# Rotary products on VectorE, early weight columns, and three smaller moves in a two-layer hybrid decoder trunk

## The chip, the core and the metric

The kernel runs on one core of a Trainium2 chip. The metric is the device time of one execution in microseconds. TensorE (PE) multiplies, VectorE (DVE), ScalarE (ACT) and GpSimd (POOL) work on tiles in SBUF, and the first two also on the accumulators in PSUM. SyncE (SP) issues most of the DMAs. An engine takes its instructions in order, and semaphores order the engines among one another.

## The reference

Two layers (DEPTH 2) on 1024 tokens of width 1024, all in float32:

```
h = RMSNorm(x); p = h @ W_in                       # columns for all branches
branch A: u * (tril(W_s) LayerNorm(v) + b) per 128-token chunk, 4 groups
branch B: window-128 attention, 8 query / 2 key heads of 64, rotary q and k, sinks
branch C: stick-breaking attention, 4 heads of 128, strictly causal
each branch * SiLU(its gate) @ its W_branch; merged with sigmoid gates from h
x <- x + RMSNorm(merged @ W_out)
```

The rotary of a head is `x1*cos - x2*sin, x2*cos + x1*sin` on its two halves.

## The kernel before

**Products.** Every operand of a large product is held as two tiles, a high part `hi` rounded to a shorter format and the rest `lo`, and `mm3` (L128 to L130) makes one product of three matmuls: hi hi, hi lo, lo hi. `split` (L111, L112) makes the pair: ScalarE casts the high part, VectorE subtracts it from the raw value. Both layers run the same program.

**Order.** The order on PE is the order of the program text, written by hand; on the other engines a scheduler orders the instructions by readiness and priority, and what stands under `tc.high_priority()` goes first. The projection of h is a stream of jobs (`proj_t` for 128 columns, 16 steps of cost 0.64, and `proj_n` for 256 columns, 64 steps of 0.32). `fill(us)` runs steps of that stream until their costs reach the sum given, `need(label)` runs it until a job is done, so that attention products and projection products alternate on PE. The jobs follow one another: branch C's columns, k and v of branch B (`kb`, `vb`), its four query pairs (`qb` 0 to 3), the gates `gb` 0 to 3, then the value columns of branch A (`va`). A job's accumulator is one of two PSUM tiles `pj`, emptied by its `evac`, which also starts what follows (`after_q`, `rope`).

**Memory.** Most of SBUF is 27 slots of 128 x 1024 words, handed out by `new()` from the head of a queue and put back at its tail by `done()`. Whoever gets a slot waits until its last user is through. Weight columns come through two buffers `wr` and six operand buffers `w` (whi, wlo, wop).

**Start.** `first_h` norms the eight token blocks of x; `norm_b` transposes a block on PE into a PSUM tile (pz), ScalarE copies it to `raw` (L238), and `split` makes both parts of h from PSUM (L239).

**Branch B.** `rope` copies the tile t with swapped halves into sw by four DMAs (L292), multiplies sw by sin and t by cos on POOL (L293, L294) and adds on VectorE (L295); then `after_q` makes hi and lo (L346, L347) and frees t. `scores` makes 4 x 256 score columns in each of two PSUM tiles (L486), from which ScalarE copies the own block (L492, L493, L498) and VectorE the previous one under a mask (L496, L499); then softmax on VectorE and ScalarE (L503 to L511, exponentials L507). `transp` transposes the weights, `attend` multiplies them with v (L543) and adds two halves (L553, L554) through a temporary slot. Scores run two blocks ahead; the numbers FB are the fills between the pieces.

**Dense part.** After branch B, `dense` computes 17 pairs of 128-column groups by a scheme of seven products for eight. `prep(p)` makes a pair's seven weight operands (wop) from the raw columns, four combinations by POOL (L748 to L758), up to six operands ahead of the products; `begin(p)` loads the raw columns as two halves, each 512 KB. VectorE adds the products (L818). Ahead of the loop stand the sums of h that the scheme needs (`Combine`) and, among its first pairs, branch A's normalisation (L615 to L621).

**End.** `project_out` multiplies by W_out in two column halves; the second pass norms each block of 128 tokens, adds x and stores it.

Of the kernel before, what the change touches and what calls it, by code (L numbers as in the profile page):

```python
# [15 lines left out]
F32 = mybir.dt.float32  # L16
# [3 lines left out]
ALU = mybir.AluOpType  # L20
AX = mybir.AxisListType

P = 128
# [10 lines left out]
O_M = 4864  # L34
NSLOT = 27
FC = (0.6, 0.6, 1.2, 0.6)
FB = (4, 1.5, 1.5, 1.8, 2.4, 2.4)
FB_MORE = {1: 2.3, 2: 1.3}


# [1 line left out]
def trunk(ctx, tc, x, w_in, gm_w_s, gm_b_s, gm_g, sinks, w_ba, w_bb, w_bc, b_merge, w_out,  # L42
# [188 lines left out]
    def norm_b(S, n, xn):  # L231

        hf, c = n // 4, (n % 4) * P
        pt = pz().rearrange("p (a b) -> p a b", a=KD)
        for k in range(KD):
            nc.tensor.transpose(pt[:, k], xn[:, k * P:(k + 1) * P], ident)
        raw = xn
        nc.scalar.copy(raw.rearrange("p (a b) -> p a b", a=KD), pt)  # L238
        split(h[hf][0][:, :, c:c + P], h[hf][1][:, :, c:c + P], pt)  # L239
        nc.sync.dma_start(S["hT"].rearrange("(k p) t -> p k t", p=P)[:, :, n * P:(n + 1) * P],  # L240
                          raw.rearrange("p (a b) -> p a b", a=KD))
        done(raw)


    def queue_layer(l, S):
# [38 lines left out]
        def rope(t):  # L284
            if "cos" not in S:
                S["cos"], S["sin"] = new(), new()
                nc.sync.dma_start(S["cos"], cos_t)
                nc.sync.dma_start(S["sin"], sin_t)
            sw = new()
            for a in range(4):  # L290
                b = a ^ 1
                nc.sync.dma_start(sw[a * 32:(a + 1) * 32, :], t[b * 32:(b + 1) * 32, :])  # L292
            nc.gpsimd.tensor_tensor(sw, sw, S["sin"], op=ALU.mult)  # L293
            nc.gpsimd.tensor_tensor(t, t, S["cos"], op=ALU.mult)  # L294
            nc.vector.tensor_tensor(t, t, sw, op=ALU.add)  # L295
            done(sw)

# [173 lines left out]
    def branch_b(l, S):  # L471
        def scores(v):
            hp, nh = divmod(v, 2)
            grp = hp // 2
            need(("qb", hp))
            qT, kk = S["qs", hp], S["kk"][grp]
            s = new()
            s3 = s.rearrange("p (c k) -> p c k", c=8)
            for q in range(2):
                z = pz().rearrange("p (c k) -> p c k", c=4)  # L480
                for j in range(2):
                    n = nh * 4 + q * 2 + j
                    k0 = max(n - 1, 0) * P
                    for e in range(2):
                        for i in range(2):
                            nc.tensor.matmul(z[:, e * 2 + j], qT[e][:, n * P:(n + 1) * P], kk[i][:, k0:k0 + 256],  # L486
                                             start=i == 0, stop=i == 1)
                sq = s3[:, q * 4:(q + 1) * 4]
                mp = mprev.bitcast(I32).unsqueeze(1)
                if nh == 0 and q == 0:  # L490

                    nc.scalar.copy(sq[:, 0::2], z[:, 0::2, :P])  # L492
                    nc.scalar.copy(sq[:, 1::2], z[:, 1::2, P:])  # L493
                    nc.gpsimd.affine_select(sq[:, 0::2], sq[:, 0::2], pattern=[[0, 2], [-1, P]], compare_op=ALU.is_ge,
                                            fill=NEG, base=0, channel_multiplier=1)
                    nc.vector.copy_predicated(sq[:, 1::2], mp.to_broadcast([P, 2, P]), z[:, 1::2, :P])  # L496
                else:
                    nc.scalar.copy(sq, z[:, :, P:])  # L498
                    nc.vector.copy_predicated(sq, mp.to_broadcast([P, 4, P]), z[:, :, :P])  # L499
            mx = sm.tile([P, 8], F32, name="mx", tag="mx", bufs=3)  # L500
            ls = sm.tile([P, 8], F32, name="ls", tag="ls", bufs=3)
            es = sm.tile([P, 8], F32, name="es", tag="es", bufs=3)
            nc.vector.tensor_reduce(mx, s3, axis=AX.X, op=ALU.max)  # L503
            nc.vector.scalar_tensor_tensor(mx, mx, -1.0, nsnk8[:, l * 4 + hp], op0=ALU.mult, op1=ALU.min)
            nc.vector.tensor_tensor(es, mx, snk8[:, l * 4 + hp], op=ALU.add)
            for c in range(8):
                nc.scalar.activation(s3[:, c], s3[:, c], AF.Exp, bias=mx[:, c:c + 1], accum_out=ls[:, c:c + 1])  # L507
            nc.scalar.activation(es, es, AF.Exp)
            nc.vector.tensor_tensor(ls, ls, es, op=ALU.add)
            nc.vector.reciprocal(ls, ls)  # L510
            nc.vector.tensor_tensor(s3, s3, ls.unsqueeze(2).to_broadcast([P, 8, P]), op=ALU.mult)  # L511
            if nh:
                done(*qT)
            return s
# [44 lines left out]
                done(o)  # L559

        need(("qb", 0))
        fill(14)
        ready = {0: scores(0)}
        fill(3)
        ready[1] = scores(1)
        fill(FB[0])
        pend = None
# [151 lines left out]
    def dense(l, S):  # L719
# [45 lines left out]
        def begin(p):  # L765

            if p < len(pairs) and p not in begun:
                begun.add(p)
                raws[p] = ([], [])
                for q in range(2):  # L770
                    if p % 2 and p > 2:
                        t = new()
                        raws[p][1].append(t)
                        t = t.rearrange("p (k c) -> p k c", k=4)
                    else:
                        t = wp.tile([P, 4, 256], F32, name="wr", tag="wr", bufs=2)
                    col = pairs[p][0]
                    nc.sync.dma_start(t, w_in[l, q * 512:(q + 1) * 512, col:col + 256]
                                      .rearrange("(k p) c -> p k c", p=P))
                    raws[p][0].append(t)  # L780
# [184 lines left out]
    def project_out(l, mg):  # L965

        gpost = new()
        nc.sync.dma_start(gpost, g_post[l].partition_broadcast(P))
        more = l + 1 < L
        if more:  # L970
            gpre = new()
            nc.sync.dma_start(gpre, g_pre[l + 1].partition_broadcast(P))
        for k in range(0, KD, 2):
            load_wo(l, 1, k)
        o0 = [new() for _ in range(4)]
        ss0 = sm.tile([P, NB], F32, name="ss0", tag="ss0", bufs=1)

        def prod(q, n):
            a = pj()
            c = slice(n * P, (n + 1) * P)  # L980
            for k in range(KD):
                mm3(a, (mg[k][0][:, c], mg[k][1][:, c]), (h[q][0][:, k], h[q][1][:, k]), k == 0, k == KD - 1)
            return a, o0[n // 2][:, (n % 2) * 512:(n % 2 + 1) * 512]

        for n in range(NB):
            a, oo = prod(0, n)
            jk = new()
            nc.scalar.activation(jk[:, :512], a, AF.Square, accum_out=ss0[:, n:n + 1])
            done(jk)
            nc.vector.tensor_tensor(oo, a, gpost[:, :512], op=ALU.mult)  # L990
        xn = {}
        last = None
        if more:
            queue_layer(l + 1, states[l + 1])
        for n in range(NB):
            a, oo = prod(1, n)
            xt, jk = new(), new()
            nc.sync.dma_start(xt, xs[l][n * P:(n + 1) * P, :])
            ss = sm.tile([P, 1], F32, name="ss2", tag="ss2", bufs=3)
            nc.scalar.activation(jk[:, :512], a, AF.Square, accum_out=ss)  # L1000
            nc.vector.tensor_tensor(ss, ss, ss0[:, n:n + 1], op=ALU.add)
            nc.vector.tensor_tensor(jk[:, 512:], a, gpost[:, 512:], op=ALU.mult)
            r, last = rms_rinv(ss)
            nc.vector.scalar_tensor_tensor(xt[:, 512:], jk[:, 512:], r, xt[:, 512:], op0=ALU.mult, op1=ALU.add)
            nc.vector.scalar_tensor_tensor(xt[:, :512], oo, r, xt[:, :512], op0=ALU.mult, op1=ALU.add)
            nc.sync.dma_start(xs[l + 1][n * P:(n + 1) * P, :], xt)
            done(jk)
            if n % 2:
                done(o0[n // 2])
            if not more:  # L1010
                done(xt)
                continue
            xn[n], last = norm_a(xt, gpre)
            if 2 <= n < 6:
                norm_b(states[l + 1], n - 2, xn.pop(n - 2))
        for t in mg:
            done(*t)
        done(gpost)
        if not more:
            return None  # L1020
        done(gpre)
        norm_b(states[l + 1], 4, xn.pop(4))
        tokens(2)
        norm_b(states[l + 1], 5, xn.pop(5))
        tokens(1)
        norm_b(states[l + 1], 6, xn.pop(6))
        tokens(1)
        norm_b(states[l + 1], 7, xn.pop(7))
        tokens(4)
        return last  # L1030
# [108 lines left out]
```

## Time and profile before

| | |
|---|---|
| median of three runs | 2069.74 us (2069.59 to 2070.36) |
| profiled execution, its own time | 2070.14 us |
| its span | 2068.4 us |
| PE busy | 2015.1 us (97%) |
| VectorE busy | 1227.0 us (59%) |
| ScalarE busy | 808.3 us (39%) |
| POOL busy | 504.3 us (24%) |
| mean granted clock of PE | 0.989 |

The span is from the first to the last instruction of one execution. A busy PE is not PE at its peak: a matmul at a granted clock of 0.50 counts as busy too. So time that could be had shows in two places, the waits of PE and the stretches with a low granted clock.

### The profile page before, as it was taken

What the parts mean: (1) busy time and instruction counts of PE and PEld (TensorE: products, weight loads), DVE (VectorE), ACT (ScalarE), POOL (GpSimd) and SP (SyncE); (2) the same over time, 40 slices, a digit from 0 to 9 for tenths busy, and PEclk for the clock granted to TensorE, in tenths of its full rate; (3) what the DMA queues carried; (4) which work ended last, traced back from release to release, by engine and by line L of the source; (5) the groups of instructions that cost most, each with busy time, mean ns of one, the idle gap of its engine ahead of it and who ended that gap; (6) DMA issues with size and microseconds to landing.
All of it is one profiled execution on the core that took longest, in us unless ns stands there. A gap on an engine that the chain in (4) does not pass through costs nothing.

```text
span 2068.4 us, 26597 instructions
## 1 busy us (share of the span) xinstructions
PE 2015.1 (97%) x10193; PEld 1688.1 (82%) x10193; DVE 1227.0 (59%) x1609; ACT 808.3 (39%) x1477; POOL 504.3 (24%) x501
## 2 busy tenths in 40 slices
PE   7999998999999999999999999989989999999998
PEld 7898886897888888888898888779978888888886
DVE  5565638567676666554546565576766666655533
ACT  6344436543234434212444344455423343432221
POOL 0221223132433220151002222231344222202500
PEclk9999998999999999999999999989999999999999
DMA  7111232223466546632441112222235655476213
GB/s 237 39 42 42 82 82 72 88 82 116 156 232 202 178 138 244 232 124 92 135 130 31 42 41 83 75 78 101 89 99 201 226 186 169 152 254 224 82 52 132
DMA packets 169055, 261.81 MB, mean 127 GB/s; under 512 B 8616, under 2 KB 122336, under 8 KB 168928
## 3 DMA queue, kind: packets, MB, share of 16 engines
q1 hardware_dynamic: 162016, 234.95, 35.0%
q10 hardware_dynamic: 6912, 25.17, 3.0%
q8 instruction: 80, 1.31, 0.3%
q14 instruction: 47, 0.39, 0.1%
HBM read 175.15 MB, written 79.69 MB: 123 GB/s over the span
## 4 chain that ended last, share of the span: by engine, by line
PE 87%; DVE 6%; ACT 3%; issue 2%; POOL 1%; DMA 1%; SPq 0%; DVEq 0%; POOLq 0%; ACTq 0%
PE pj L130 16%; PE pj L129 16%; PE pj L128 16%; PE pz L130 6%; PE pz L128 5%; PE pz L129 5%; PE ptr L130 5%; PE ptr L128 5%; PE ptr L129 5%; PE ptr L413 1%; PE pz L486 1%; PE pav L543 1%; PE pav L129 1%; DVE s L112 1%; PE pav L130 1%
## 5 line engine op out<-in xcount | busy, mean ns | idle before, releaser
L128 PE MATMUL pj<-h,whi 128*128 128x512 f32 x700 | 287.1, 410 | 9.2 <-ACT s L257 9.2
L129 PE MATMUL pj<-h,whi 128*128 128x512 f32 x700 | 279.1, 399 | 0.0
L130 PE MATMUL pj<-h,wlo 128*128 128x512 f32 x700 | 278.6, 398 | 0.0
L128 PEld LDWEIGHTS pj<-h,whi 128*128 128x128 f32 x700 | 133.6, 191 | 35.0 <-ACT s L257 10.1
L130 PEld LDWEIGHTS pj<-h,wlo 128*128 128x128 f32 x700 | 132.9, 190 | 32.0
L129 PEld LDWEIGHTS pj<-h,whi 128*128 128x128 f32 x700 | 133.3, 190 | 23.5
L112 DVE TENSOR_TENSOR wlo<-wr,whi 128x1024 fp32r<-128x1024 f32 x80 | 107.0, 1340 | 72.2 <-ACT whi L111 72.1
L128 PE MATMUL pj<-whi,h 128*128 128x256 f32 x512 | 148.5, 290 | 1.2 <-ACT h L111 1.2
L111 ACT CAST whi<-wr 128x1024 fp32r<-128x1024 f32 x80 | 84.0, 1050 | 159.8 <-PE pj L129 104.1
L130 PE MATMUL pj<-whi,h 128*128 128x256 f32 x512 | 144.4, 282 | 1.8 <-DVE h L112 1.8
L129 PE MATMUL pj<-wlo,h 128*128 128x256 f32 x512 | 144.1, 281 | 0.1
L940 POOL TENSOR_TENSOR s<-s,s 128x512 f32<-128x512 f32 x56 | 81.4, 1457 | 223.8 <-DVE s L934 197.9
L111 ACT CAST wop<-wr 128x512 fp32r<-128x512 f32 x120 | 73.1, 617 | 149.6 <-DMA wr<-in_w_in_dram 34.5
L112 DVE TENSOR_TENSOR wop<-wr,wop 128x512 fp32r<-128x512 f32 x120 | 101.4, 848 | 41.9 <-ACT wop L111 41.7
L396 DVE TENSOR_TENSOR_SCAN s<-s,ones 128x128 f32<-128x128 f32 (+3 forms) x64 | 87.6, 1369 | 63.5 <-POOL s L391 63.3
L111 ACT CAST wop<-s 128x512 fp32r<-128x512 f32 x118 | 71.9, 618 | 122.2 <-PE pz L130 43.7
L112 DVE TENSOR_TENSOR s<-ptr,s 128x512 fp32r<-128x512 f32 (+2 forms) x132 | 77.2, 589 | 66.5 <-ACT s L111 66.0
L112 DVE TENSOR_TENSOR wop<-s,wop 128x512 fp32r<-128x512 f32 x118 | 97.8, 834 | 12.2 <-ACT wop L111 11.8
L129 PE MATMUL pj<-h,s 128*128 128x512 f32 x256 | 102.0, 398 | 0.0
L128 PE MATMUL pj<-h,s 128*128 128x512 f32 x256 | 101.1, 395 | 0.0
L130 PE MATMUL pj<-h,s 128*128 128x512 f32 x256 | 100.6, 393 | 0.0
L130 PEld LDWEIGHTS pj<-whi,h 128*128 128x128 f32 x512 | 97.1, 190 | 2.7 <-DVE h L112 2.7
(230 smaller groups left out, 5176.9 us busy)
## 6 DMA issues: line engine op xcount, KB each, us to landing
wr<-in_w_in_dram SPq DMA_DIRECT2D x96, 512.0 KB, 4.0
sg<-s ACTq DMA_DIRECT2D x48, 512.0 KB, 5.1
s<-sg SPq DMA_DIRECT2D x48, 512.0 KB, 4.9
s<-in_w_in_dram SPq DMA_DIRECT2D x28, 512.0 KB, 5.1
s<-in_x_dram SPq DMA_DIRECT2D x16, 512.0 KB, 4.1
hT<-s SPq DMA_DIRECT2D x16, 512.0 KB, 3.2
s<-hT SPq DMA_DIRECT2D x16, 512.0 KB, 3.8
wor<-in_w_out_dram SPq DMA_DIRECT2D x16, 512.0 KB, 3.7
```

Of the source, the lines that this page charges most:

```text
L111: nc.scalar.copy(hi, raw)
L112: nc.vector.tensor_tensor(lo, raw, hi.bitcast(F32), op=ALU.subtract)
L128: nc.tensor.matmul(acc, lh, rh, start=first, stop=False)
L129: nc.tensor.matmul(acc, lh, rl, start=False, stop=False)
L130: nc.tensor.matmul(acc, ll, rh, start=False, stop=last)
L396: nc.vector.tensor_tensor_scan(t1[:, :kl][:, ::-1], t1[:, :kl][:, ::-1], ones.to_broadcast([P, kl]), 1.0, op0=ALU.mult, op1=ALU.mult)
L413: nc.tensor.transpose(pt[:, b - b0], t2[:, b * P:(b + 1) * P], ident)
L486: nc.tensor.matmul(z[:, e * 2 + j], qT[e][:, n * P:(n + 1) * P], kk[i][:, k0:k0 + 256], start=i == 0, stop=i == 1)
L543: nc.tensor.matmul(av[:, j], w, t.rearrange("p (e j) k -> p e j k", j=2)[:, :, j], start=i == 0, stop=i == len(ops) - 1)
L940: eng.tensor_tensor(acc[dm][:, ts], acc[dm][:, ts], sg[:, ts], op=ALU.add)
```

## The change

Six edits. In `norm_b`, for the first layer alone, POOL casts the high part of h from the copy in SBUF, and VectorE subtracts from that copy instead of from PSUM. In `rope` both products run on VectorE, cos first. In branch B's `scores` the copies of the scores out of PSUM stand under high priority. The fills of branch B get other numbers. In `begin`, pair 1's raw columns go to slots, as those of the odd pairs from 3 on did, instead of to the two buffers `wr`. In `project_out` the two multiply-adds change places, and the last layer stores each half of a block by itself, the first by SP's queue and the second by ScalarE's.

```diff
--- before.py
+++ after.py
@@ -34,7 +34,7 @@
 O_M = 4864
 NSLOT = 27
 FC = (0.6, 0.6, 1.2, 0.6)
-FB = (4, 1.5, 1.5, 1.8, 2.4, 2.4)
+FB = (5, 1.4, 1.4, 1.7, 2.2, 2.2)
 FB_MORE = {1: 2.3, 2: 1.3}
 
 
@@ -236,7 +236,13 @@
             nc.tensor.transpose(pt[:, k], xn[:, k * P:(k + 1) * P], ident)
         raw = xn
         nc.scalar.copy(raw.rearrange("p (a b) -> p a b", a=KD), pt)
-        split(h[hf][0][:, :, c:c + P], h[hf][1][:, :, c:c + P], pt)
+        if S is states[0]:
+
+            r3 = raw.rearrange("p (a b) -> p a b", a=KD)
+            nc.gpsimd.tensor_copy(h[hf][0][:, :, c:c + P], r3)
+            nc.vector.tensor_tensor(h[hf][1][:, :, c:c + P], r3, h[hf][0][:, :, c:c + P].bitcast(F32), op=ALU.subtract)
+        else:
+            split(h[hf][0][:, :, c:c + P], h[hf][1][:, :, c:c + P], pt)
         nc.sync.dma_start(S["hT"].rearrange("(k p) t -> p k t", p=P)[:, :, n * P:(n + 1) * P],
                           raw.rearrange("p (a b) -> p a b", a=KD))
         done(raw)
@@ -290,8 +296,8 @@
             for a in range(4):
                 b = a ^ 1
                 nc.sync.dma_start(sw[a * 32:(a + 1) * 32, :], t[b * 32:(b + 1) * 32, :])
-            nc.gpsimd.tensor_tensor(sw, sw, S["sin"], op=ALU.mult)
-            nc.gpsimd.tensor_tensor(t, t, S["cos"], op=ALU.mult)
+            nc.vector.tensor_tensor(t, t, S["cos"], op=ALU.mult)
+            nc.vector.tensor_tensor(sw, sw, S["sin"], op=ALU.mult)
             nc.vector.tensor_tensor(t, t, sw, op=ALU.add)
             done(sw)
 
@@ -487,16 +493,17 @@
                                              start=i == 0, stop=i == 1)
                 sq = s3[:, q * 4:(q + 1) * 4]
                 mp = mprev.bitcast(I32).unsqueeze(1)
-                if nh == 0 and q == 0:
-
-                    nc.scalar.copy(sq[:, 0::2], z[:, 0::2, :P])
-                    nc.scalar.copy(sq[:, 1::2], z[:, 1::2, P:])
-                    nc.gpsimd.affine_select(sq[:, 0::2], sq[:, 0::2], pattern=[[0, 2], [-1, P]], compare_op=ALU.is_ge,
-                                            fill=NEG, base=0, channel_multiplier=1)
-                    nc.vector.copy_predicated(sq[:, 1::2], mp.to_broadcast([P, 2, P]), z[:, 1::2, :P])
-                else:
-                    nc.scalar.copy(sq, z[:, :, P:])
-                    nc.vector.copy_predicated(sq, mp.to_broadcast([P, 4, P]), z[:, :, :P])
+                with tc.high_priority():
+                    if nh == 0 and q == 0:
+
+                        nc.scalar.copy(sq[:, 0::2], z[:, 0::2, :P])
+                        nc.scalar.copy(sq[:, 1::2], z[:, 1::2, P:])
+                        nc.gpsimd.affine_select(sq[:, 0::2], sq[:, 0::2], pattern=[[0, 2], [-1, P]], compare_op=ALU.is_ge,
+                                                fill=NEG, base=0, channel_multiplier=1)
+                        nc.vector.copy_predicated(sq[:, 1::2], mp.to_broadcast([P, 2, P]), z[:, 1::2, :P])
+                    else:
+                        nc.scalar.copy(sq, z[:, :, P:])
+                        nc.vector.copy_predicated(sq, mp.to_broadcast([P, 4, P]), z[:, :, :P])
             mx = sm.tile([P, 8], F32, name="mx", tag="mx", bufs=3)
             ls = sm.tile([P, 8], F32, name="ls", tag="ls", bufs=3)
             es = sm.tile([P, 8], F32, name="es", tag="es", bufs=3)
@@ -559,9 +566,9 @@
                 done(o)
 
         need(("qb", 0))
-        fill(14)
+        fill(12)
         ready = {0: scores(0)}
-        fill(3)
+        fill(5)
         ready[1] = scores(1)
         fill(FB[0])
         pend = None
@@ -768,7 +775,7 @@
                 begun.add(p)
                 raws[p] = ([], [])
                 for q in range(2):
-                    if p % 2 and p > 2:
+                    if p % 2:
                         t = new()
                         raws[p][1].append(t)
                         t = t.rearrange("p (k c) -> p k c", k=4)
@@ -1001,9 +1008,14 @@
             nc.vector.tensor_tensor(ss, ss, ss0[:, n:n + 1], op=ALU.add)
             nc.vector.tensor_tensor(jk[:, 512:], a, gpost[:, 512:], op=ALU.mult)
             r, last = rms_rinv(ss)
+            nc.vector.scalar_tensor_tensor(xt[:, :512], oo, r, xt[:, :512], op0=ALU.mult, op1=ALU.add)
+            if not more:
+                nc.sync.dma_start(xs[l + 1][n * P:(n + 1) * P, :512], xt[:, :512])
             nc.vector.scalar_tensor_tensor(xt[:, 512:], jk[:, 512:], r, xt[:, 512:], op0=ALU.mult, op1=ALU.add)
-            nc.vector.scalar_tensor_tensor(xt[:, :512], oo, r, xt[:, :512], op0=ALU.mult, op1=ALU.add)
-            nc.sync.dma_start(xs[l + 1][n * P:(n + 1) * P, :], xt)
+            if more:
+                nc.sync.dma_start(xs[l + 1][n * P:(n + 1) * P, :], xt)
+            else:
+                nc.scalar.dma_start(xs[l + 1][n * P:(n + 1) * P, 512:], xt[:, 512:])
             done(jk)
             if n % 2:
                 done(o0[n // 2])
```

## Rows read from the trace of the kernel before

**Rows 1.** Waits of TensorE: waiter, awaited, us in total, times, longest.

```profile
PE pj L128 <- ACT s L257: 9.2, 2, 4.9
PE pz L486 <- DVE s L499: 8.1, 2, 4.1
PE ptr L130 <- DVE wop L112: 5.3, 2, 3.0
PE pj L130 <- DVE wop L112: 2.9, 2, 2.4
PE pz L130 <- DVE wop L112: 2.7, 2, 2.2
PE pj L130 <- DVE h L112: 1.8, 4, 0.7
```

**Rows 2.** Stretches: length, busy us of PE, PEld, DVE, ACT, POOL, granted clock, DMA.

```profile
323.91:329.98 6.07, 6.07 (x22) 5.56 (x23) 6.07 (x7) 1.94 (x7) 3.52 (x3) 0.50 0.36 101
358.33:364.07 5.74, 5.74 (x16) 4.57 (x17) 3.10 (x4) 0.59 (x1) 1.27 (x2) 0.50 0.56 181
487.00:490.22 3.22, 3.22 (x9) 2.54 (x8) 0.56 (x2) 0.28 (x1) 0.22 (x1) 0.50 0.55 163
497.00:501.00 4.00, 4.00 (x12) 3.17 (x11) 2.18 (x5) 0.62 (x1) 2.44 (x1) 0.57 0.61 148
...
1345.80:1351.90 6.10, 6.10 (x25) 5.61 (x26) 6.10 (x7) 1.96 (x7) 3.54 (x3) 0.61 0.35 98
1380.13:1386.00 5.87, 5.87 (x18) 4.77 (x19) 3.10 (x4) 0.59 (x1) 1.27 (x2) 0.61 0.54 178
1508.00:1512.00 4.00, 4.00 (x13) 3.08 (x12) 1.08 (x4) 0.06 (x1) 0.00 (x0) 0.62 0.50 137
1518.00:1522.50 4.50, 4.50 (x13) 3.60 (x14) 2.68 (x5) 0.62 (x1) 3.40 (x1) 0.64 0.39 116
```

**Rows 3.** Timeline of ScalarE in branch B: start, duration, instruction, idle before.

```profile
321.43 1.05 ACT L498 COPY s<-pz 128x512 f32<-128x512 f32 x2
```

**Rows 4.** Timeline of POOL and VectorE around the second rotary.

```profile
311.81 2.40 POOL L294 TENSOR_TENSOR s<-s,s 128x1024 f32<-128x1024 f32 x1
...
312.31 1.92 DVE L504 SCALAR_TENSOR_TENSOR mx<-mx,nsnk 128x8 f32<-128x8 f32 x1
314.27 0.17 DVE L505 TENSOR_TENSOR es<-mx,snk 128x8 f32<-128x8 f32 x1
```

**Rows 5.** Timeline of SP, POOL and VectorE, the last rotary of branch B.

```profile
339.65 2.42 SPq L292 DMA_DIRECT2D s<-s  x4
...
343.95 2.98 POOL L293 TENSOR_TENSOR s<-s,s 128x1024 f32<-128x1024 f32 x1 [4.74 <-DMA s<-s]
...
349.56 1.23 DVE L295 TENSOR_TENSOR s<-s,s 128x1024 f32<-128x1024 f32 x1
...
356.44 1.22 DVE L347 TENSOR_TENSOR s<-s,s 64x1024 fp32r<-64x1024 f32 x1
```

**Rows 6.** Stretches where VectorE is full, columns as in rows 2.

```profile
325.00:350.00 25.00, 25.00 (x126) 21.39 (x126) 23.89 (x29) 15.45 (x51) 14.16 (x9) 0.90 0.30 85
...
482.00:487.00 5.00, 2.76 (x13) 1.93 (x12) 4.80 (x14) 2.12 (x3) 1.29 (x1) 1.00 0.25 105
```

**Rows 7.** Timeline of SP, VectorE and ScalarE at the dense part's start.

```profile
486.17 0.37 SPq L778 DMA_DIRECT2D wr<-in_w_in_dram  x1
...
490.74 4.54 DVE L621 TENSOR_SCALAR s<-s,mv,rs 128x512 f32<-128x512 f32 x7
...
492.76 0.62 ACT L111 CAST wop<-wr 128x512 fp32r<-128x512 f32 x1 [2.19 <-POOL wr L751]
```

**Rows 8.** One line's durations (min/median/max ns); a group by form (busy, mean).

```profile
L526 POOL TENSOR_SCALAR_AFFINE_SELECT s<-s x64: 637/638/1681, 334.1 to 1481.2; 128x512 fp32r<-128x512 f32 x64
...
L111 ACT CAST h<-pz 128x1024 fp32r<-128x1024 f32 x16 | 16.3, 1021 | 0.0
```

**Rows 9.** DMA issues of the output: KB each, median us to landing.

```profile
out_dram<-s SPq DMA_DIRECT2D x8, 512.0 KB, 2.7
```


## The prediction

> **What bounds the kernel now.** I read the table of waits for TensorE first, since TensorE is busy in nearly all of the span: only a wait that stops it, or a lower clock, can be won back. The reader is to see that there are few such waits and that each stands once in each layer. Three places matter, and I call them A, B and C.
>
> A: the score products L486 wait 8.1 us in two waits. B: the projection products L128 wait 9.2 us in two for the copy L257. C: products of the dense part wait for the low halves of weight operands (wop, L112) on three tiles, 5.3 + 2.9 + 2.7 = 10.9 us in six waits [rows 1].
>
> Then the table by stretches. The granted clock was 0.50, the 1.2 GHz level, for 6.07 us behind A, for 5.74 behind B, for 3.22 behind the middle wait of C, and 0.57 over 4.00 us behind its last [rows 2]. Work at 1.2 GHz loses half of its time, so what is lost is length times (1 - granted clock): 3.0, 2.9, 1.6 and 1.7. The second layer's four stretches give 2.4 (6.10 x 0.39), 2.3, 1.5 and 1.6 [rows 2]. With the idle time, A costs 8.1 + 5.4 = 13.5 us in the kernel, B 9.2 + 5.2 = 14.4, C 10.9 + 6.4 = 17.3. In all 45.2 us: the pool from which this change can draw, beside 1.8 us in which the first layer's products wait for h [rows 1].
>
> Last the order on the other engines, which says why PE waits.
>
> **A, score copies put first.** The scores of block 1 are copied out of PSUM by ScalarE at 321.43, and PE stands for 4.1 us, until 323.91, since block 2 wants that PSUM tile back [rows 1 to 3]. ScalarE was working through block 0's exponentials. With the high-priority block these copies go ahead of them. Each costs 0.5 us on ScalarE (1.05 for two [rows 3]) and must be made anyway; moved forward, the pair delays the exponentials by 1.05 us. I take all of A: +13.5 (bounds 0, if something else holds block 2, and 13.5).
>
> **The fills.** A fill runs steps of 0.64 until its sum is used up, so 14 and 12 are 22 and 19 steps, 3 and 5 are 5 and 8, and FB[0] 4 and 5 are 7 and 8: one step more ahead of the loop. In the loop 1.5/1.4, 1.8/1.7 and 2.4/2.2 are the same 3, 3 and 4 steps while the filler comes in steps of 0.64; with the value columns' 0.32, 2.4 becomes 7 steps instead of 8. So the total of PE's work is as before, and 8 short steps (2.6 us by the kernel's own costs) move behind branch B, in front of the dense part. The first scores start three steps, 1.9 us, sooner. They need rotary done sooner.
>
> **B, rotary on VectorE.** Two POOL products of 2.40 become two VectorE products of 1.23, if they cost what the add L295 of the same shape costs [rows 4, 5]: the chain of one rotary is 2.34 shorter, which covers the 1.9. In B's chain the four swaps are issued from 339.65, POOL starts at 343.95 and needs 2.98 for the first product, the add starts at 349.56, and the last low half L347 ends at 357.66 [rows 5]; only then is the slot free into which gate b0's first half is copied. The products will take 2.46 there instead of about 5.4, so the chain ends 2.9 sooner.
>
> A second effect comes from the fills. Going through the slot queue by hand, gate b0's first half falls at step 8, which before came after the attend of block 0's second half and now comes before it. So it takes the swap tile's slot, free after the add (350.8 in this trace, 6.9 us before the other [rows 5]), and the attend's temporary takes the rotary tile's slot. The attend's accumulator is wanted back a transpose pair later, so some of the wait may turn up there.
>
> VectorE pays: 2.46 us more for each rotary, and it is busy 23.89 of 25 us from 325 on [rows 6]. But it gets time back. L504 on 8 columns took 1.92 us, from 312.31 until 314.23, and POOL's rotary product ended at 314.21; the next such tiny operation took 0.17 [rows 4]. Three late rotaries are six POOL products in the stretch of A and B; if four of them hold a tiny operation for 1.75 us, as this one did, that is 7 us (an estimate). Against the three late rotaries' 7.4 that is even. So VectorE stays full and I take 11 of B's 14.4 (bounds 0 and 14.4). I also take off 2 us for the two first scores coming before their operands (bounds 0 and 2 x 4: an early start of 1.9 lost, and a clock fall like the 1.6 to 1.7 of C's [rows 2]).
>
> The Trainium skill, GPSIMD Engine Reference, Key points, says that GpSimd shares its SBUF interfaces with VectorE and contends with VectorE instructions that have two SBUF inputs. The row of L504 agrees; by the rule, too, the change takes ten POOL products out of VectorE's way in each layer and puts new contention at the start, where h's subtraction now reads two SBUF tiles.
>
> **C, early columns for the second pair.** In C's last wait the second half of pair 1's columns is loaded into a weight buffer that is freed only when pair 0's operands are made: issue at 486.17, then POOL, then ScalarE at 492.76, then VectorE behind seven normalisations that start at 490.74 and take 4.54 [rows 7]. With slots of their own the two loads can be issued when branch B's value slots are free, some 20 us sooner, and the chain stands well ahead of the products. Two slots are free then (9 of 27 by my count). SP issues two loads as before, only earlier. I take C's last wait whole: its idle 2.4 + 3.0 [rows 1] and clock 1.7 + 1.6 [rows 2] make 8.7. C's middle wait is pair 0's own last operand, behind a full VectorE (4.80 of 5.00 [rows 6]); the 2.6 us of filler moved in front help it, and pair 1's low halves compete with it: half of 2.2 + 2.2 + 1.6 + 1.5 = 7.5, 3.8 (bounds 0 and 7.5). The first wait, about a half microsecond, stays. Against this stand pair 1's four POOL products, which now fall into that full stretch and can hold VectorE's two-input work: 2 us a layer, -4 (bounds 0, and four of 1.3 us a layer, -10.4).
>
> **Start, h by POOL.** No row shows POOL copying 1024 elements. A one-input operation on 512 takes 0.638, twice that is 1.28; the two-input product takes 2.40; ScalarE's cast took 1.02 [rows 4, 8]. I take 1.3, the one-input operation being the nearest. ScalarE loses eight casts, and it stood in the way of the copies; the chain copy, cast, subtract grows by 0.3 for a tile. Bounds: all of the 1.8 us won, or eight times 1.38, 11.0, lost. I take +0.5.
>
> **End, halves by two queues.** A store of 512 KB takes 2.7 us from issue to landing [rows 9]. The first half now leaves one multiply-add sooner, the second is half as large and leaves when the whole left before. Between 0 and half of 2.7: +0.6. The order of the two multiply-adds changes nothing else.
>
> **The sum.** 13.5 + 11 - 2 + 8.7 + 3.8 - 4 + 0.5 + 0.6 = 32.1 us. The profiled execution took 2070.14 with a span of 2068.4, 0.4 above the median of 2069.74: 2070.1 - 32.1 = 2038.0.
>
> **The rivals.**
>
> Only A goes (0.15). B's wait moves to the attend's temporary, C's to pair 0's last operand. For it: VectorE is full in both places. Against it: the chain of B is 2.9 shorter and the load of C 20 us earlier. 2070.1 - 13.5 - 0.6 = 2056.
>
> The start gets worse (0.05). POOL's cast and the two-input subtraction wait for one another, and a POOL fill that waits for a store stands in front of a cast. 11.0 lost instead of 0.5 won: 2049.5.
>
> Nothing is won (0.05). VectorE is full behind A too, so that PE, let through at A, waits as long a little later: within 4 us of 2069.
>
> Slower (0.07). VectorE works in order. If the rotary product stands at its head before the swaps have landed, it waits there up to the 4.3 us between the first swap's issue and POOL's start [rows 5], with copies and low halves behind it. Three rotaries a layer lie in the full stretch: 12.9 us idle and 7.4 of products, less 5.3 given back, 15 a layer. If A and B stay for that reason and the 15 come on top, 2070.1 + 30 - 9.6 = 2090.5, the 9.6 being C, start and end. It decides from 9.6 / 6 = 1.6 us a rotary on. Against it: on POOL the same wait stood before the same loads, and VectorE has nothing ready in front of the first two rotaries.
>
> **Numbers.** My forecast has 0.68; its own range is from all 45.2 + 1.8 + 1.3 won, 2022, to a sum without C's 8.7 and with B at half, 2051. About 0.2%, 4 us, is what a measurement of this kernel can tell from no change. All but the last two rivals are faster: 0.88; same 0.05; slower 0.07. The range from 2024 to 2061 leaves out the top of the first case and the last two.
>
> **What would show it.** A: the waits of L486 for L499 gone, L498's copies within 2 us of their products, the clock near 1.00 from 320 to 345. B: L257's wait gone or under 2 us; rotary products of 1.2 us on VectorE, L504 at 0.17. C: the last wait for wop gone, pair 1's loads issued some 20 us sooner. Start: POOL casts of 1.0 to 1.4. I am wrong if VectorE's rotary products sit behind long waits for DMA, if a new wait of 3 us or more stands at the first scores, at the attend of block 0 or at pair 0's last operand, or if POOL's cast takes over 2 us.

## The result and the profile after

The changed kernel takes 2045.78 us (median of four runs, 2045.12 to 2046.52) beside 2069.9 for the kernel before in the same comparison: a ratio of 0.9883, 95% interval 0.9871 to 0.9896. 24 us are won where 32.1 were forecast; the time lies inside the forecast's range, 2024 to 2061. The profiled execution has a span of 2044.8 us instead of 2068.4, PE busy 2005.2 us, and a mean granted clock of 0.997 instead of 0.989.

In the changed kernel `rope` is L299 to L301, the end of `after_q` L352 and L353, the score products L492, the score copies L505 and L506, the tiny softmax operations L511 and L512, gate b0's copy L263, h's parts L242 and L243.

Waits of TensorE after, columns as in rows 1, behind a first line that both kernels have nearly alike (the transposes L236, 9.0 us here and 8.9 before):

```profile
PE pz L492 <- DVE s L353: 7.0, 4, 2.9
PE pav L129 <- DVE s L112: 6.2, 12, 1.2
PE pj L130 <- DVE h L243: 3.1, 3, 1.4
PE pj L128 <- ACT s L263: 2.0, 2, 1.0
PE pz L130 <- DVE wop L112: 1.7, 2, 1.3
PE ptr L526 <- DVE s L561: 1.7, 2, 0.8
PE pj L130 <- DVE wop L112: 1.3, 1, 1.3
...
PE ptr L130 <- DVE wop L112: 0.4, 1, 0.4
```

Stretches after, columns as in rows 2:

```profile
311.15:317.00 5.85, 5.85 (x26) 5.34 (x27) 2.31 (x4) 1.24 (x3) 0.41 (x1) 0.71 0.04 12
320.00:345.00 25.00, 25.00 (x139) 21.49 (x138) 21.70 (x32) 22.28 (x69) 5.59 (x5) 1.00 0.24 59
352.00:365.00 13.00, 12.02 (x64) 9.89 (x63) 10.28 (x17) 9.86 (x29) 3.07 (x3) 1.00 0.20 75
490.00:502.00 12.00, 12.00 (x55) 9.77 (x54) 11.21 (x15) 2.49 (x4) 6.06 (x4) 1.00 0.14 43
...
1318.00:1322.00 4.00, 2.59 (x10) 2.30 (x11) 2.12 (x2) 0.83 (x2) 0.00 (x0) 0.52 0.52 145
1322.00:1328.00 6.00, 6.00 (x25) 5.11 (x24) 4.24 (x5) 1.72 (x4) 0.41 (x1) 0.75 0.02 4
```

Beside [rows 1, 2], A, B and C are clean. The 8.1 us for the score copies are gone, the copy of gate b0 costs 2.0 instead of 9.2, the weight operands 3.4 instead of 10.9, and the clock behind each place is at 1.00. What is new is the first line: 7.0 us at the first scores, 3.65 in layer 1 and 3.36 in layer 2, and behind them the only low clock left while PE still multiplies.

Timelines of VectorE, ScalarE and TensorE after, at the first scores of layer 1 (start, duration, instruction, idle before and releaser):

```profile
298.55 1.22 DVE L299 TENSOR_TENSOR s<-s,s 128x1024 f32<-128x1024 f32 x1 [2.38 <-DMA s<-s]
299.69 1.22 DVE L300 TENSOR_TENSOR s<-s,s 128x1024 f32<-128x1024 f32 x1
305.08 1.23 DVE L112 TENSOR_TENSOR wlo<-wr,whi 128x1024 fp32r<-128x1024 f32 x1 [4.16 <-ACT whi L111]
306.22 1.22 DVE L301 TENSOR_TENSOR s<-s,s 128x1024 f32<-128x1024 f32 x1
308.62 2.47 DVE L353 TENSOR_TENSOR s<-s,s 64x1024 fp32r<-64x1024 f32 x2 [1.19 <-ACT s L352]
```

```profile
304.00 1.05 ACT L111 CAST whi<-wr 128x1024 fp32r<-128x1024 f32 x1 [4.77 <-PE pj L129]
...
309.90 0.51 PE L492 MATMUL pz<-s,s 128*128 128x256 f32 x2 [2.90 <-DVE s L353]
311.15 3.33 PE L492 MATMUL pz<-s,s 128*128 128x256 f32 x14 [0.75 <-DVE s L353]
```

Both products are done at 300.9, but the add, which needs nothing else, starts at 306.22. Ahead of it in VectorE's queue stands the low half of the next projection weights, and that waits for its high half, which ScalarE can cast only at 304.00, when PE gives an operand buffer back. VectorE idles 4.16 us with the add ready behind it. The Trainium skill (PSUM — Partial Sum Buffer, Engine vs sequencer instructions) says that VectorE's queue is strictly first in, first out; these rows agree.

### The profile page after: what moved, and what is told of

Read it like the earlier page. It is cut to its first block, busy times and chain, and to the rows that moved or that the text cites. A ratio compares the mean times of both kernels' runs of the same rounds, so it can differ in the third digit from the quotient of the medians.

```text
span 2044.8 us, 26597 instructions
## 1 busy us (share of the span) xinstructions
PE 2005.2 (98%) x10193; PEld 1679.8 (82%) x10193; DVE 1243.2 (61%) x1629; ACT 800.0 (39%) x1469; POOL 473.8 (23%) x489
## 4 chain that ended last, share of the span: by engine, by line
PE 87%; DVE 7%; ACT 2%; issue 2%; POOL 1%; DMA 1%; SPq 0%; DVEq 0%; POOLq 0%; ACTq 0%
PE pj L128 16%; PE pj L130 16%; PE pj L129 16%; PE pz L130 6%; PE pz L129 6%; PE pz L128 6%; PE ptr L130 5%; PE ptr L129 5%; PE ptr L128 5%; PE ptr L419 1%; PE pz L492 1%; PE pav L129 1%; PE pav L550 1%; DVE s L112 1%; PE pav L130 1%
## 5 line engine op out<-in xcount | busy, mean ns | idle before, releaser
L112 DVE TENSOR_TENSOR wlo<-wr,whi 128x1024 fp32r<-128x1024 f32 x80 | 108.1, 1353 | 85.8 <-ACT whi L111 85.7
L111 ACT CAST wop<-s 128x512 fp32r<-128x512 f32 x130 | 78.6, 618 | 129.1 <-PE ptr L130 43.7
L112 DVE TENSOR_TENSOR wop<-wr,wop 128x512 fp32r<-128x512 f32 x108 | 94.8, 878 | 34.0 <-ACT wop L111 33.9
L112 DVE TENSOR_TENSOR wop<-s,wop 128x512 fp32r<-128x512 f32 x130 | 107.6, 838 | 12.7 <-ACT wop L111 12.2
L112 DVE TENSOR_TENSOR s<-ptr,s 128x512 fp32r<-128x512 f32 (+2 forms) x132 | 77.3, 589 | 58.4 <-ACT s L111 57.7
L111 ACT CAST wop<-wr 128x512 fp32r<-128x512 f32 x108 | 65.8, 617 | 109.8 <-PE ptr L130 27.3
```

The costliest lines, as they stand in the source:

```text
L111: nc.scalar.copy(hi, raw)
L112: nc.vector.tensor_tensor(lo, raw, hi.bitcast(F32), op=ALU.subtract)
```

## The experiments

Each time stands beside that of the kernel before, and the diffs, with what is left out marked by dots, are against the kernel named. The kernel before took 2069.74 to 2070.89 us beside these kernels, so a difference of about 1 us between two of them tells nothing. Line numbers in the rows are those of the kernel that ran.

### The order at the first scores

The changed kernel, with one constraint in `load_w`, which loads and splits a job's weights: on VectorE, a low half may not stand ahead of the rotary add that belongs in front of it (`adds` collects the adds).

```diff
...
-        split(hi, lo, raw)
+        if len(adds) > 1:
+            with tc.issue_after(adds[-2].ins):
+                split(hi, lo, raw)
+        else:
+            split(hi, lo, raw)
...
-            nc.vector.tensor_tensor(t, t, sw, op=ALU.add)
+            adds.append(nc.vector.tensor_tensor(t, t, sw, op=ALU.add))
```

> The changed kernel, with one ordering edge: VectorE's low half of the weights loaded next (wlo) may not stand ahead of the rotary add of the query pair before. Theory of the queue: the new 2.9 us wait at the first scores comes from that low half, which waits for a weight slot with the finished add behind it; ScalarE's weight cast still stands ahead of the rotary casts, so about half of the wait goes: the first wait falls from 2.9 to about 0.5 us in each layer, and the time from 2045.8 to about 2038. Rival, the fills are too short: the operands would be late in any order, the wait stays within 0.5 us of 2.9, and so does the time.

Measured: 2038.32 us (2037.52 to 2039.23), ratio 0.9847 (0.9833 to 0.9862). The first scores wait 3.5 instead of 7.0. Then the whole chain is put first, on VectorE and on ScalarE: the next weights' cast and low half, and the second copy of the next query pair, come behind the last cast and subtraction of `after_q` (collected as `chains`):

```diff
...
-        split(hi, lo, raw)
+        if len(chains) > 1:
+            cast, low = chains[-2]
+            with tc.issue_after(cast.ins), tc.issue_after(low.ins):
+                split(hi, lo, raw)
+        else:
+            split(hi, lo, raw)
...
-                nc.scalar.mul(S[nm][:, hf * HT:(hf + 1) * HT], acc, sc)
+                if hf and chains:
+                    with tc.issue_after(chains[-1][0].ins):
+                        nc.scalar.mul(S[nm][:, hf * HT:(hf + 1) * HT], acc, sc)
+                else:
+                    nc.scalar.mul(S[nm][:, hf * HT:(hf + 1) * HT], acc, sc)
...
```

> The changed kernel, with the whole rotary chain (ScalarE's two casts and VectorE's two subtractions) ordered ahead of the next weights' cast and low half and of the next query pair's second copy. Theory of the queue: the chain ends about 2 us before the first scores, all four waits there (7.0 us) and the low clock behind them go, about 11 us: 2035. Rival, the fills are too short: a wait of over 1 us stays at the first scores. A further possibility: pushing the other copies back makes the scores of the second pair wait instead, and less than half of the 11 us is won.

Measured: 2035.6 us (2034.97 to 2036.18), ratio 0.9833 (0.9817 to 0.985); the first scores wait 0.9 in all. VectorE's timeline of this kernel, and a stretch of it with columns as in rows 2:

```profile
299.69 1.22 DVE L311 TENSOR_TENSOR s<-s,s 128x1024 f32<-128x1024 f32 x1
302.11 2.47 DVE L363 TENSOR_TENSOR s<-s,s 64x1024 fp32r<-64x1024 f32 x2 [1.20 <-ACT s L362]
305.38 1.23 DVE L113 TENSOR_TENSOR wlo<-wr,whi 128x1024 fp32r<-128x1024 f32 x1 [0.81 <-ACT whi L112]
```

```profile
304.00:316.00 12.00, 12.00 (x69) 10.42 (x68) 7.27 (x10) 7.35 (x21) 0.41 (x1) 1.00 0.36 88
```

The add follows the products at once, the low half comes last, and no wait of TensorE is left that names it. The order of the chain is worth 10.2 us: 7.5 by the low half that may no longer stand ahead of the add on VectorE, the rest by the order behind the add. With the first constraint alone the subtraction at 305.74 still waits 3.38 us for ScalarE's cast; here it waits 1.20, at 302.11.

### Where the rotary products run

The changed kernel with the products back on POOL:

```diff
-            nc.vector.tensor_tensor(t, t, S["cos"], op=ALU.mult)
-            nc.vector.tensor_tensor(sw, sw, S["sin"], op=ALU.mult)
+            nc.gpsimd.tensor_tensor(sw, sw, S["sin"], op=ALU.mult)
+            nc.gpsimd.tensor_tensor(t, t, S["cos"], op=ALU.mult)
```

> The changed kernel with the two rotary products back on POOL. Theory, the rotary chain is what the first scores and gate b0 wait for: with products of 2.4 instead of 1.2 us the first scores wait 2.5 to 4 us a layer and the wait for gate b0's copy grows by 2 us or more a layer, 2050 to 2060. Rival, VectorE is full and the products cost there what they save in the chain: the time stays within 3 us of 2045.8, and tiny VectorE operations take 1.7 to 2 us again.

Measured: 2044.72 us (2044.25 to 2044.89), ratio 0.9875 (0.986 to 0.989). My expectation fails and the rival holds: the move to VectorE wins nothing that can be told in the changed kernel. With POOL's products the add happens to stand ahead of the low half again, and the first scores wait 3.1 instead of 7.0; in return the attend waits for VectorE and POOL, 3.9 in all, and the tiny operations are held again. Two groups of this kernel's VectorE by form (busy, mean ns), then its timeline of POOL and VectorE:

```profile
L511 DVE SCALAR_TENSOR_TENSOR mx<-mx,nsnk 128x8 f32<-128x8 f32 x16 | 9.6, 601 | 0.3
...
L512 DVE TENSOR_TENSOR es<-mx,snk 128x8 f32<-128x8 f32 x16 | 2.6, 162 | 0.3
```

```profile
329.69 2.39 POOL L300 TENSOR_TENSOR s<-s,s 128x1024 f32<-128x1024 f32 x1
...
329.77 2.33 DVE L511 SCALAR_TENSOR_TENSOR mx<-mx,nsnk 128x8 f32<-128x8 f32 x1
```

So I asked the same with the chain put first, where nothing can come between: the kernel of 2035.6 with the same two lines on POOL.

> The changed kernel with the rotary's chain put first (measured 2035.6), but with both rotary products back on POOL. Theory (VectorE's rotary is worth something as soon as nothing stands between its operations, since each product takes 1.23 instead of 2.40 us): the first scores wait 3 us or more again, products of the attend wait some 3 us for POOL and VectorE as they did in the kernel with only the products moved back; 2041 to 2044 us. Rival (the order on VectorE was all; where the products run is nothing): 2035 to 2037 us, with waits like those of the kernel it is made from.

Measured: 2042.61 us (2041.48 to 2042.97), ratio 0.9871 (0.9853 to 0.9888). The time and the attend's wait are as the theory has them: in the right order VectorE's products are worth 7.0 us, and without them the attend waits 3.1 us again. The first scores are not: they wait 1.8 us, not 3 or more, and gate b0's copy 3.8 instead of 3.1. In the order of the changed kernel the products make no difference that can be told (1.1 us the other way). And the kernel before with this one edit, the two lines on VectorE:

> The kernel before with one edit: both rotary products on VectorE, cos first. The prediction's step (B is won by a rotary that ends 2.9 us sooner): the wait for gate b0's copy goes from 9.2 to under 4 us, 2059 to 2063 us. Theory now (gate b0's copy waits for a slot that the fills hand out, and the shorter products only shorten that wait a little, while the next weights' low half can come between the products and the add): waits for gate b0's copy of 3 to 8 us, new waits of the first scores; 2062 to 2070 us.

Measured: 2065.45 us (2061.88 to 2066.9), ratio 0.9978 (0.9968 to 0.9988). The time fits the theory, and so do new waits of 3.1 us at the first scores; the wait for gate b0's copy does not, 12.4 us where 9.2 stood before [rows 1]. A reason is in ScalarE's timeline:

```profile
315.84 0.59 ACT L498 COPY s<-pz 128x512 f32<-128x512 f32 x1 [3.14 <-PE pz L486]
316.80 0.59 ACT L498 COPY s<-pz 128x512 f32<-128x512 f32 x1 [0.37 <-PE pz L486]
...
320.84 0.40 ACT L507 ACTIVATE s<-s,mx 128x128 f32<-128x128 f32 x1
```

Without any priority the scheduler here put the score copies ahead of the exponentials, and A's 8.1 us are gone in this kernel too. So the priority is not the only edit that wins A, and PE, let through at A, waits longer at B, as in the next kernel.

### What held gate b0's copy

The kernel before with the score copies under high priority, nothing else:

```diff
+                with tc.high_priority():
-                if nh == 0 and q == 0:
+                    if nh == 0 and q == 0:
...
```

> The kernel before, with the high priority for the copies of the scores alone. By the prediction's step A: the waits of the score products for the masked copies (8.1 us) and the low clock behind them go, 13.5 us: 2056, with the other waits as they were. Rival, VectorE is full and another wait takes its place: less than 5 us won.

Measured: 2065.99 us (2064.8 to 2068.01), ratio 0.9981 (0.9972 to 0.9991): 4 us where 13.5 were expected. Its waits of TensorE, TensorE's timeline in layer 1, and the stretch behind that wait:

```profile
PE pj L128 <- ACT s L257: 15.6, 2, 8.0
```

```profile
357.23 0.80 PE L128 MATMUL pj<-h,whi 128*128 128x512 f32 x1 [7.63 <-ACT s L257]
```

```profile
357.23:363.00 5.77, 5.77 (x18) 4.66 (x19) 1.92 (x3) 0.59 (x1) 1.27 (x2) 0.61 0.60 182
```

A's wait is gone, and B's has grown by 6.4: PE stands at B from 349.60 instead of 353.96, and the copy starts at 356.60 instead of 357.69, since it comes no sooner than the chain's end allows. To see what ties it to that end, the changed kernel with one thing more, gate b0's first half in the queue's second slot instead of its first, PE's order unchanged:

```diff
-                if hf == 0:
+                if hf == 0 and (br, c) == ("b", 0):
+                    first = free.popleft()
+                    ev.g = new()
+                    free.appendleft(first)
+                elif hf == 0:
```

> The changed kernel, where gate b0's first half takes the second slot of the queue instead of the first; so it again gets the slot of the last rotary tile, and the attend's temporary the swap tile's. PE's order is unchanged. Theory, the slot decides B: the two waits for gate b0's copy grow from 2.0 us together to 6 or more, with a low clock behind them, 2052 to 2058. Rival, the shorter chain alone did it: under 3 us of waits and a time within 2 us of 2045.8.

Measured: 2058.67 us (2058.63 to 2059.5), ratio 0.9944 (0.9929 to 0.9958): 12.9 us lost against the changed kernel, a little more than expected, and TensorE waits 11.2 us at B. And the priority together with the fills, which hand out the slots, in the kernel before:

```diff
-FB = (4, 1.5, 1.5, 1.8, 2.4, 2.4)
+FB = (5, 1.4, 1.4, 1.7, 2.2, 2.2)
...
-        fill(14)
+        fill(12)
...
-        fill(3)
+        fill(5)
```

> The kernel before with two edits, the score copies under high priority and the new fills; nothing on VectorE, columns as before. Alone, the priority gave 4 us, since the wait for gate b0's copy grew by what the score copies won. Theory (the priority pays as soon as the fills hand gate b0 another slot; the two together give A and most of B, and the fills C's middle wait): the waits for the score copies and for gate b0's copy are under 4 us together, C's last wait stays; 2046 to 2052 us. Rival (B needs the shorter rotary too, and the two edits only add up their small gains): 2060 to 2066 us, with 8 us or more of waits for gate b0's copy.

Measured: 2049.79 us (2048.72 to 2050.12), ratio 0.9904 (0.9888 to 0.992). Two edits that move no work between engines give 20.1 us, where all six give 24.1. How the 20.1 divide between the two is open: the new fills alone were not run. Gate b0's copy and the last operations of the last rotary's chain (for the changed kernel with the swaps' issue ahead), in the timelines of the changed kernel, of the one with swapped slots, and of the one with these two edits:

```profile
339.57 2.42 SPq L298 DMA_DIRECT2D s<-s  x4
...
353.15 1.22 DVE L301 TENSOR_TENSOR s<-s,s 128x1024 f32<-128x1024 f32 x1
...
354.40 0.59 ACT L263 COPY s<-pj 128x512 f32<-128x512 f32 x1 [3.16 <-DVE s L301]
...
356.10 2.47 DVE L353 TENSOR_TENSOR s<-s,s 64x1024 fp32r<-64x1024 f32 x2 [0.41 <-ACT s L352]
```

```profile
357.14 1.22 DVE L357 TENSOR_TENSOR s<-s,s 64x1024 fp32r<-64x1024 f32 x1
358.46 0.69 DVE L263 COPY s<-pj 128x512 f32<-128x512 f32 x1
358.81 0.56 ACT L267 COPY s<-pj 128x512 f32<-128x512 f32 x1
...
359.21 0.80 PE L128 MATMUL pj<-h,whi 128*128 128x512 f32 x1 [5.59 <-DVE s L263]
```

```profile
348.04 1.23 DVE L295 TENSOR_TENSOR s<-s,s 128x1024 f32<-128x1024 f32 x1
...
351.40 0.58 ACT L257 COPY s<-pj 128x512 f32<-128x512 f32 x1
...
354.93 1.22 DVE L347 TENSOR_TENSOR s<-s,s 64x1024 fp32r<-64x1024 f32 x1
```

Followed through the slot queue of each program: where gate b0 has the rotary tile's slot, its first copy starts the moment the last low half ends, at 357.69 in the kernel before, 356.60 with the priority alone, 354.26 with VectorE's products alone. With the slots swapped VectorE's copy of the second half (L263 there) comes first, at 358.46, and ScalarE's of the first half (L267) at 358.81. Where gate b0 has the swap tile's slot, the copy starts behind the add, at 354.40, or, where ScalarE is busy with exponentials until then, at 351.40, three and a half microseconds before the last low half starts.

### Fills and columns

The changed kernel with the fills of before:

> The changed kernel with the fills of before. Theory of the queue: the low half is behind the end of the second query pair on PE, which the fills don't move, so the chain ends at the same time after that pair and the first scores, 1.9 us later, still wait 1 to 1.7 us; at the end of branch B, 8 short steps fewer stand in front of the dense part and the middle wait for its operands grows by 1 to 2 us a layer. Time 2040 to 2047. Rival, the fills are too short: no wait at the first scores, time 2034 to 2037.

Measured: 2053.42 us (2052.87 to 2053.93), ratio 0.992 (0.9905 to 0.9935). 7.6 us lost, more than expected. Gate b0's copy waits 8.3 again and C's middle wait is back, 2.24 us at 483.84 in layer 1; the first scores, started three steps later, wait 3.1 instead of 7.0; C's last wait stays gone. The kernel before with pair 1's columns in slots:

```diff
-                    if p % 2 and p > 2:
+                    if p % 2:
```

> The kernel before, with the early columns for the second pair alone. By the prediction's step C: the last wait for weight operands (2.4 and 3.0 us) and the low clock behind it go, the middle wait (2.2 us a layer) stays, since nothing moves in front of it: 2061. Rival, the middle wait swallows it because pair 1's low halves now compete with pair 0's last: the middle wait grows to 3 us or more and less than 4 us is won.

Measured: 2062.43 us (2060.78 to 2063.1), ratio 0.9958 (0.9941 to 0.9975). C's last wait is gone and its middle wait stays, 2.24 at 488.03. New are 2.8 us of waits for low halves of h (L112). The two halves of C have separate causes: columns for the last, fills for the middle, by the prediction's count the eight short steps moved in front.

### The start

The kernel before with the high part of h by POOL:

> The kernel before with one edit: in the first layer POOL casts the high part of h, and VectorE subtracts from the copy in SBUF. The prediction's step: 0.5 us won (bounds 1.8 won, 11 lost), 2069.2 us. Theory now, from the trace of the changed kernel (a POOL cast of up to 1.68 us beside VectorE's two-input norms stands in front of the first product's operand): 1 to 2 us lost, 2070.5 to 2071.5 us, and 3 us of waits for h instead of 1.8.

Measured: 2070.8 us (2069.32 to 2072.7), ratio 1.0005 (0.9995 to 1.0014): no difference that can be told. The waits for h are 3.1 as expected. The kernel of 2035.6 with h's parts made as before:

> The kernel with the whole rotary chain ordered first (2035.6), with the first layer's high part of h back on ScalarE. Theory, the cast on POOL costs time at the start, since two norms on VectorE and the cast hold one another: the products' waits for h fall from 3.1 to 1.8 us and the time by 1 to 2 us, to 2034. Rival, it relieves ScalarE as meant: the time rises by 1 us or more.

Measured: 2034.95 us (2034.73 to 2035.61), ratio 0.9829 (0.9814 to 0.9843), the lowest median of all. The waits for h go from 3.1 to 1.8; that POOL's casts lose about 1 us rests on these waits and on the trace, since both differences of time are about as large as the spread of the runs. Timelines of VectorE and POOL of the changed kernel, at the start:

```profile
26.09 3.27 DVE L227 SCALAR_TENSOR_TENSOR s<-s,r,s 128x1024 f32<-128x1024 f32 x2
29.28 1.21 DVE L243 TENSOR_TENSOR h<-s,h 128x1024 fp32r<-128x1024 f32 x1
...
26.61 1.68 POOL L242 CAST h<-s 128x1024 fp32r<-128x1024 f32 x1 [2.65 <-ACT s L238]
30.12 1.28 POOL L242 CAST h<-s 128x1024 fp32r<-128x1024 f32 x1 [1.84 <-ACT s L238]
```

POOL's cast takes 1.68 us beside two normalisations with two SBUF inputs, which take 3.27 together where one alone took 1.28 at 21.05; three casts later on took 1.04. These rows agree, on both engines, with the rule of the Trainium skill that the prediction weighed (GPSIMD Engine Reference, Key points).

## Why the prediction was right and wrong

The direction was right and the forecast 7.8 us too low. The step that failed is the smallest term of the part on B, the 2 us taken off for first scores that come before their operands. One of the prediction's own signs of being wrong stands there, a new wait of 3 us or more at the first scores: 3.65 and 3.36. That the total came within 8 us is partly luck, since C won 5.4 more than its terms and the first scores cost 9.4 more than theirs.

**First scores, -2.** By the rows they cost 7.0 of idle time, 5.85 x 0.29 = 1.7 of clock in layer 1, and 2.59 x 0.48 + 6.00 x 0.25 = 2.7 in layer 2: 11.4 in all. The mechanism was foreseen, scores started before the rotary is done; its size was bounded at 8 by three steps of earlier start, with no thought of what the scheduler puts between a product and its add. The kernel with the chain first gives 10.2 back.

**A, +13.5.** The wait is gone and the clock from 320 to 345 is 1.00. But the term is not a gain by itself: the priority alone gave 4 us, because B's copy waited for a chain with an end of its own. Nor is it the priority's alone: with VectorE's products alone the wait is gone too. My rival "only A goes", 2056, added the terms as if they were free of one another, and so did the sum.

**B, +11.** 14.4 less 2.0 for the copy and 1.7 for the attend's temporary, which the prediction named, leaves 10.7. The size is right, the first reason is wrong. The chain does not end 2.9 sooner: from the swaps' issue to the end of the last low half it is 19.0 us, 339.57 to 358.57, where it was 18.0 before, 339.65 to 357.66 [rows 5]; and the add starts at 353.15, later than with POOL's products in the kernel with priority and fills, 348.04. What was put as a second effect, the slot that the fills hand to gate b0, was most of it. VectorE's products add less at this place: without them, in the kernel with priority and fills, the copy waits 3.0 instead of 2.0 and the attend 3.9 more.

**VectorE stays full.** From 320 to 345 it is busy 21.70 of 25 us. The tiny operations are free again, L511 at a mean of 216 ns, in the kernel before 862. What the held operations cost is not shown: the kernel with POOL's products spends 9.6 us in L511 against 3.5, for a time that cannot be told from the changed kernel's, but its first scores also wait less.

**C, +8.7 + 3.8 - 4.** 7.5 of idle time and all of the 6.4 of clock are won, 13.9, where the terms made 8.5. The last wait is gone, and the middle one fell from 2.24 to 0.38 us in each layer, by the fills. But the first, which was to stay at half a microsecond, is 1.28. TensorE in layer 1 after:

```profile
474.02 0.50 PE L130 MATMUL pz<-s,wop 128*128 128x512 f32 x1 [1.28 <-DVE wop L112]
480.25 0.50 PE L130 MATMUL ptr<-h,wop 128*128 128x512 f32 x1 [0.38 <-DVE wop L112]
```

In the kernel with priority and fills alone neither of these two waits is there; in the changed kernel they are there with either engine's products. So they are most likely the price of the early columns, 3.3 us for both layers, near the 4 taken off.

**Start and end, +0.5 and +0.6.** The first h phase ends at 48.24 instead of 46.93: -1.3. The casts took 1.04 to 1.68, 1.3 was a fair mean; that each would also slow the normalisation beside it was left out. From PE's last product to the end of the span it is 6.31 instead of 6.83: +0.5, as said; no kernel was run with this edit alone.

The title names the rotary and the columns and counts the rest as smaller moves; of the six edits it was the priority and the fills that won most. With these sizes the sum is 13.5 + 10.7 - 11.4 + 13.9 - 1.3 + 0.5 = 25.9 for a difference of 23.6 between the spans; 2.3 I cannot assign. The rival of VectorE's queue blocked at its head came true in kind, though not behind swaps and not in the full stretch: behind an operand buffer, at the rotary of the first query pair, where I had written that VectorE has nothing ready in front.

## What to carry to other kernels

When an operation moves to a queue that is in order, look at what a scheduler may put between its steps, and above all for an operation that waits for a third engine: here one low half ahead of one add cost 7.5 us, 10.2 with the order of the rest of the chain, and hid the whole worth of the faster engine. Waits that follow one another on the bottleneck engine are not added up: removing the first pays only if what ends the second moves too, so test edits also in the pairs in which they free the path, and each of the pair alone. Where buffers are handed out by a queue, a change of order changes which buffer each step gets, and through it what the step waits for.

## What the runs showed of the hardware

- In the changed kernel with POOL's products, POOL held VectorE's 128x8 operation until its own product ended: 2.33 us from 329.77 to 332.10, POOL's product from 329.69 to 332.08, where the same operation takes 166 ns at the median.
- A store of half the bytes did not take half the time: 2.0 us for 256 KB where 512 KB took 2.7 [rows 9]:

```profile
out_dram<-s SPq DMA_DIRECT2D x8, 256.0 KB, 2.0
out_dram<-s ACTq DMA_DIRECT2D x8, 256.0 KB, 2.0
```

- A wait of TensorE of the same length did not always cost clock. Behind 2.24 us at 483.84 in the changed kernel with the old fills the clock was 1.00 over 4.16 us; behind 2.24 us at 488.03 in the kernel with early columns alone it was 0.66 over 4.97. Why is open. Behind waits of 0.98 (L263 after) and 1.57 us (the kernel with priority and fills) it stayed at 1.00.
